# A decoder layer on one core: banded scores of two key parts in one matmul, gate loads issued a step earlier, and weight sums, a merge and the last feature's products put elsewhere

## The chip, the cores and the metric

The kernel runs on one core of a Trainium2 chip. A core has a matrix engine (TensorE, PE in the profile, with its weight loads as PEld), a vector engine (VectorE, DVE), a scalar engine (ScalarE, ACT), a general engine (GpSimd, POOL), a queue engine that issues most of the transfers (SyncE, SP), and sixteen DMA engines. Data lies in the on-chip memory SBUF, matmul results in PSUM, everything else in DRAM. The metric is the time of one execution on the device in microseconds (us); less is better.

## The reference

One layer of a decoder over 1024 tokens of width 1024, in float32, with 3 x 4 heads of dilated window attention beside 4 heads of differential attention, and a gated feed-forward part with a short causal convolution:

```python
h = rms_norm(x, pre_mix_g)
qa, ka, va, qb, kb, vb, gates = split(h @ w_in)          # 1024 x (512*3 + 1536*3 + 2048)
ya = (rms_norm(diff_attention(rope(qa), rope(ka), va, lam), diff_head_g) * (1 - lam_init)) @ w_a_out
for g, (window, dil) in enumerate(((128, 1), (512, 4), (2048, 16))):
    outs[g], lses[g] = dilated_group(rope(qb[g]), rope(kb[g]), vb[g], window, dil)
yb = sum_g(softmax_over_g(lses)[g] * outs[g]) @ w_b_out
g_a, g_b = split(sigmoid(gates))
x = x + rms_norm((g_a * ya + g_b * yb) @ w_mix_out, post_mix_g)
u = causal_depthwise_conv(rms_norm(x, pre_ffn_g) @ w_up, conv_w, conv_b)     # 2 x 2816 columns
x = x + rms_norm((gelu(gate(u)) * value(u)) @ w_down, post_ffn_g)
```

`dilated_group` lets a query see the keys at its distance 0, dil, 2 dil ... up to `window`. On each residue class this is a band in blocks of 128 keys: the query's own block and the one before it.

## The kernel before, in words

**Precision.** Every operand of a large matmul is kept as two tiles: a high part (a ScalarE copy that rounds, L149) and a low part (a VectorE subtraction of that from the source, L146). A product is three matmuls into one PSUM region (`mm3`, L155 to L157): high by high, low of the first by high, high of the first by low of the second. PE is so the engine that is always wanted, and ACT and DVE split, scale and drain for it.

**Order.** The work goes through the stages below, and inside them a planner (`interleave`, `later`, `due`) hands out pieces: attention of one step is interleaved with the projections of the next one; a piece put off with `later(n, ...)` is issued n matmul jobs later. Each engine then runs its own list in the order of issue and waits only where an operand or a buffer is not there.

1. Norms, tables, values, and attention A with its projections, up to about 500 us.
2. Attention B, about 505 to 855 us, in twelve steps of (pair, group g, head h), each over 4 pairs of query blocks (`attend_b`). Group 0 has keys of two blocks for nearly all query blocks, group 1 for every second one, group 2 (whose residue classes are folded in twos) always one block of 128. Scores of a pair stand in one PSUM bank `s`; DVE adds the mask and takes the largest (L992), ACT takes the exponential (L998), PE turns the result (L713), and ACT and DVE copy it into two parts; PE multiplies with the values (L725, L727) and ACT and DVE drain (`osb`, L1026 and L1027). Queries and keys of the next step come from `proj_b`: DVE turns them by the rotary tables, and ACT and DVE write the parts `qh`, `ql`, `kh`, `kl` (L894 and L895), one half of the sequence at a time. Where a step opens a new group, `between` splits that group's values into `vh` and `vl` between the query's and the key's projections. `put_stats` has PE turn a step's row sums for DRAM, with a copy `rows` on ACT (L1050).
3. Branch A output, about 855 to 925 us: `branch` loads weight units, loads two gate tiles ahead (`gl<-gt_d`, on POOL's queue), takes their sigmoid on ACT (L1188), and DVE multiplies each product by its gate (`ya`, L1210). Beside it run the pieces of the last heads' merge over groups (`merge`: loads of `mw` and `og`, one DVE product of 1536 columns, L1106, two sums L1107 and L1109), at the job numbers of the tuple (3, 5, 7, 11, 16).
4. Branch B output and the mix, then the up projection. Features 2 to 21 each take seven products of 12 matmuls (`seven`) in place of eight. Four of the seven weights are sums of weight quarters: `combined` starts a tile `s` and adds the others by DMAs on POOL's queue (L1408); `weights` then splits each into parts. The `s` tiles have four buffers, all four of one feature. Products p1, p2, p3 and p5 take the second operand straight out of the mix tiles `mh`, `ml`, products p6, p7 and p4 out of the separate tiles `t2`, `t3`, `t4`. Results go to `u` (L1446 first), through the convolution, and as `c` to DRAM (`c_d`).
5. The down projection, from about 1470 us, again by sevens: `load(n)` brings `ax` from `c_d` (L1570) and `by` from the weights (L1571) for the product "p1"; their places in SBUF are those of tiles that the up projection has used, `by`'s among them those of the mix tiles. Matmuls there are L1618 to L1620.

## Time and profile before

| what | us |
|---|---|
| three runs | 1689.71, 1692.87, 1689.78 |
| their median | 1689.78 |
| the profiled execution, its own time | 1693.0 |
| span of the profile (first to last instruction) | 1691.1 |
| PE busy / DVE busy / ACT busy / POOL busy | 1672.0 / 1318.6 / 923.9 / 161.9 |
| mean granted TensorE clock | 0.997 |

The profile is one execution. What a row of the timeline shows: start, duration, engine, line, operation, and output<-inputs by the program's names; in square brackets the time that the engine stood idle just before and what it waited for. Matmuls overlap, so what one costs is the distance from its start to the next one's start, not its duration. The 1.9 us between 1691.1 and 1693.0 lie around the span.

### The profile page before, as it was taken

Reading aid. Unit: us, or ns where it says so; the run is one execution under the profiler, and the core shown is the slowest. Engines: PE = TensorE matmul, PEld = TensorE weight load, DVE = VectorE, ACT = ScalarE, POOL = GpSimd, SP = SyncE. Lnnn points to the kernel's source line nnn. Section 1 sums busy time; section 2 is a strip of 40 time slices with the busy share of each in tenths; the row PEclk is TensorE's granted clock in tenths of the full one; section 3 lists DMA queues with packets and bytes.
Section 4 is the critical chain, followed back from the end, with each engine's and each line's share of the span. In section 5 each row is a group of like instructions: output and inputs, shape, how many; then the busy total and the mean of one; then the engine's idle time right before and its main releaser. Section 6 shows DMA issues by size and latency. Waiting matters only on the chain. (4 is left out here: it accounts for less than half of the span.)

```text
span 1691.1 us, 22909 instructions
## 1 busy us (share of the span) xinstructions
PE 1672.0 (99%) x7878; PEld 1395.7 (83%) x7878; DVE 1318.6 (78%) x2446; ACT 923.9 (55%) x1723; POOL 161.9 (10%) x251
## 2 busy tenths in 40 slices
PE   9999999999999999999999999999999999999997
PEld 7888888888888888888878888888888888878886
DVE  8794686877777777788866865988888778689978
ACT  7643575655554777667653533565555455255463
POOL 0031000000000000010123400022211121000000
PEclk9999999999999999999999999999999999999999
DMA  8777311214112122333676632267655655296524
GB/s 273 228 248 245 98 59 61 88 57 121 48 63 81 55 72 77 107 120 119 208 257 215 203 112 87 51 162 171 163 132 133 154 134 128 98 338 214 197 88 149
DMA packets 115973, 237.40 MB, mean 140 GB/s; under 512 B 14272, under 2 KB 23424, under 8 KB 115856
## 3 DMA queue, kind: packets, MB, share of 16 engines
q1 hardware_dynamic: 89296, 171.28, 30.4%
q0 software_dynamic: 21808, 56.26, 14.2%
q10 hardware_dynamic: 4752, 8.39, 1.3%
q8 instruction: 62, 1.02, 0.2%
q14 instruction: 55, 0.45, 0.1%
HBM read 177.54 MB, written 47.86 MB: 133 GB/s over the span
## 5 line engine op out<-in xcount | busy, mean ns | idle before, releaser
L157 PE MATMUL acc<-xl,whi 128*128 128x512 f32 x768 | 303.2, 395 | 0.0
L155 PE MATMUL acc<-xh,whi 128*128 128x512 f32 x768 | 302.1, 393 | 0.0
L156 PE MATMUL acc<-xh,wlo 128*128 128x512 f32 x768 | 301.9, 393 | 0.0
L149 ACT ACTIVATE whi<-raw 128x512 fp32r<-128x512 f32 (+1 forms) x249 | 153.9, 626 | 162.6 <-PE acc L157 94.2
L146 DVE TENSOR_TENSOR wlo<-raw,whi 128x512 fp32r<-128x512 f32 (+1 forms) x249 | 171.9, 698 | 27.8 <-ACT whi L149 23.5
L156 PEld LDWEIGHTS acc<-xh,wlo 128*128 128x128 f32 x768 | 144.6, 188 | 28.2
L157 PEld LDWEIGHTS acc<-xl,whi 128*128 128x128 f32 x768 | 144.6, 188 | 28.0
L155 PEld LDWEIGHTS acc<-xh,whi 128*128 128x128 f32 x768 | 144.7, 188 | 27.5
L155 PE MATMUL acc<-mh,whi 128*128 128x512 f32 x384 | 149.7, 390 | 1.4 <-ACT u L1446 1.1
L156 PE MATMUL acc<-mh,wlo 128*128 128x512 f32 x384 | 149.4, 389 | 0.0
L157 PE MATMUL acc<-ml,whi 128*128 128x512 f32 x384 | 149.1, 389 | 0.0
L700 ACT ACTIVATE t<-acc 64x512 f32<-64x512 f32 (+1 forms) x160 | 94.6, 591 | 60.1 <-PE acc L157 58.2
L149 ACT ACTIVATE whi<-s 128x512 fp32r<-128x512 f32 x80 | 49.8, 627 | 90.8 <-PE acc L157 68.7
L1442 DVE TENSOR_TENSOR u<-acc,u 128x512 f32<-128x512 f32 x100 | 68.4, 685 | 28.4 <-PE acc L157 28.2
L701 DVE TENSOR_TENSOR t<-acc,cos 128x512 f32<-128x512 f32 x64 | 44.2, 690 | 59.4 <-ACT t L700 58.9
L155 PEld LDWEIGHTS acc<-mh,whi 128*128 128x128 f32 x384 | 72.1, 188 | 17.4 <-ACT u L1446 2.0
L157 PEld LDWEIGHTS acc<-ml,whi 128*128 128x128 f32 x384 | 72.1, 188 | 15.0
L156 PEld LDWEIGHTS acc<-mh,wlo 128*128 128x128 f32 x384 | 72.1, 188 | 14.7
L1619 PE MATMUL acc<-whi,wlo 128*128 128x512 f32 x216 | 76.0, 390 | 0.0
L1618 PE MATMUL acc<-whi 128*128 128x512 f32 x216 | 74.9, 390 | 0.3 <-ACT whi L149 0.3
L1620 PE MATMUL acc<-wlo,whi 128*128 128x512 f32 x216 | 71.6, 390 | 0.0
L793 ACT ACTIVATE s<-s,mx 128x896 f32<-128x896 f32 (+7 forms) x64 | 49.3, 771 | 35.1 <-DVE mx L786 18.8
(403 smaller groups left out, 4033.9 us busy)
## 6 DMA issues: line engine op xcount, KB each, us to landing
raw<-in_w_in SPq DMA_DIRECT2D x96, 256.0 KB, 2.9
raw<-in_w_v SPq DMA_DIRECT2D x71, 256.0 KB, 5.0
raw<-in_w_up SPq DMA_DIRECT2D x68, 256.0 KB, 3.5
raw<-c_d SPq DMA_DIRECT2D x48, 256.0 KB, 3.7
c_d<-c SPq DMA_DIRECT2D x22, 512.0 KB, 3.9
s<-in_w_up POOLq DMA_DIRECT2D x40, 256.0 KB, 4.1
s<-s POOLq DMA_DIRECT2D x40, 256.0 KB, 3.9
raw<-in_w_down SPq DMA_DIRECT2D x37, 256.0 KB, 3.6
```

The costliest lines, as they stand in the source:

```text
L146: eng.tensor_tensor(lo, src, hi.bitcast(F32), op=ALU.subtract)
L149: copy = nc.scalar.activation(hi, src, AF.Copy)
L155: nc.tensor.matmul(o, sh, mh, start=first, stop=False, skip_group_check=on)
L156: nc.tensor.matmul(o, sl, mh, start=False, stop=False, skip_group_check=on)
L157: nc.tensor.matmul(o, sh, ml, start=False, stop=last, skip_group_check=on)
L700: nc.scalar.activation(t1[dst], ps[src], AF.Copy)
L701: nc.vector.tensor_tensor(t2, ps, cos[:, sl], op=ALU.mult)
L793: exp = nc.scalar.activation(sc[c][:, :w], sc[c][:, :w], AF.Exp, bias=mx[:, c, 0:1], scale=-1.0, accum_out=den[:, c : c + 1])
L1442: nc.vector.tensor_tensor(to, made(p), x, op=ALU.add)
L1618: nc.tensor.matmul(banks[m], gh[:, tk], wh, start=f == 0, stop=False)
L1619: nc.tensor.matmul(banks[m], gl[:, tk], wh, start=False, stop=False)
L1620: nc.tensor.matmul(banks[m], gh[:, tk], wl, start=False, stop=f == NH - 1)
```

## The change

It has six parts.

- **Scores.** For groups 1 and 2 the high and the low part of the keys lie in one tile `kp` of the shape (128, 2, 512), two such tiles for the two halves of the sequence. Where a query block has one key block, one matmul of the high query part over both (256 columns, L1009) and one of the low query part over the high keys (128 columns, L1010) take the place of the three of 128 columns. The columns of high by low then lie beside the others in PSUM; a new DVE addition (`low`, L1017) adds the mask to them, and the result stands in the place of the mask in the old reduction. Two-block scores and group 0 keep `mm3`. With two tiles, the key copies (L905 and L906) are issued for each half of a tile apart: four of 256 columns in place of two of 512, on ACT and on DVE.
- **Keys ahead.** The key copies are issued at a higher priority where the step has value splits. On ACT the order at the first such place stays: `vh_5509`, an `osb`, a `pt`, the `rows` copy, `vh_5513`, and then the key copies, four of them now and two before; DVE likewise has `vl` ahead of them.
- **Gates.** The first two gate tiles of branch A are loaded ahead of the last step of attention B and handed to `branch`. POOL's order of transfers around them is the one of before.
- **Merge.** The fourth number of the tuple goes from 11 to 12.
- **Weight sums.** Of odd features the four sums are made in one tile of the pool `early`, of even ones in the four `s` buffers. On POOL the sums of feature 4 now stand ahead of those of feature 3.
- **Last feature.** Its products go p1, p2, p3, p5, p6, p7, p4 (`LAST_UP` gives the weights in that order); before they went p1, p6, p2, p7, p5, p4, p3.

```diff
@@ -46,6 +46,7 @@
 NH = NF // 2
 AHEAD, T1_AT, LAST = 4, 5, 7
+LAST_UP = ("a11", "a12", "s4", "s1", "s2", "s3", "a22")
 MIX_UNITS = {3: (0,), 4: (1,), 5: (2, 4), 6: (5,), 7: (6, 3, 7)}
 START_GATES, A_FILLS, B_GATES = 1, ("gpgg", "gpvgg", "wgpgg", "xgPVgg"), 3
 SLOTS = 18
@@ -883,22 +884,38 @@
     def proj_b(g, h, res, between=None):
         dil = DIL[g]
-        qh, ql, kh, kl = (slot(n) for n in ("qh", "ql", "kh", "kl"))
-        res += [qh, ql, kh, kl]
+        qh, ql = (slot(n) for n in ("qh", "ql"))
+        if g == 0:
+            keys = [tuple(slot(n) for n in ("kh", "kl"))]
+        else:
+            keys = [slot("kp", (P, 2, 512)) for _ in range(2)]
+        res += [qh, ql, keys]
         n = 512 // dil
-        def put(hi, lo):
+        def pair_of(t):
+            return t if isinstance(t, tuple) else (t[:, 0], t[:, 1])
+
+        def put(*tiles):
             def evacuate(half, sl, ps):
                 t = rotated(ps, *tabs_b, sl, 64).rearrange("p (i r) -> p r i", r=dil)
-                o, l = (t_.rearrange("p (r i) -> p r i", r=dil)[:, :, half * n : (half + 1) * n] for t_ in (hi, lo))
-                nc.scalar.activation(o, t, AF.Copy)
-                nc.vector.tensor_tensor(l, t, o.bitcast(F32), op=ALU.subtract)
+                m = dil // len(tiles)
+                for x, pair in enumerate(tiles):
+                    o, l = (t_.rearrange("p (r i) -> p r i", r=m)[:, :, half * n : (half + 1) * n] for t_ in pair_of(pair))
+                    from_ = t[:, x * m : (x + 1) * m]
+                    nc.scalar.activation(o, from_, AF.Copy)
+                    nc.vector.tensor_tensor(l, from_, o.bitcast(F32), op=ALU.subtract)
             return evacuate
-        yield from proj_t(QB + g * 512 + h * P, put(qh, ql))
+        yield from proj_t(QB + g * 512 + h * P, put((qh, ql)))
         if between:
             between()
-        yield from proj_t(KB + g * 512 + h * P, put(kh, kl))
+        evacuate = put(*keys)
+
+        def first(*at):
+            with tc.high_priority(offset=80 if between else 0):
+                evacuate(*at)
+
+        yield from proj_t(KB + g * 512 + h * P, first)
     steps = [(pair, g, h) for pair in range(2) for g in range(BG) for h in (2 * pair, 2 * pair + 1)]
     ops_b = {s: [] for s in steps}
@@ -966,7 +983,7 @@
     def attend_b(g, h, jj, ops, vs, sbs):
-        qh, ql, kh, kl = ops
+        qh, ql, keys = ops
         scale = P ** -0.5
         if jj == 0:
             sbs.append(wk_b[0].tile([P, S], F32, tag="osb", name="osb", bufs=1))
@@ -980,17 +997,32 @@
             spans.append((j, kb, at))
             at += len(kb) * P
         ps = psum(F32, ps_s, "s")
-        for j, kb, a0 in spans:
-            w, k = slice(a0, a0 + len(kb) * P), slice(kb[0] * P, (j + 1) * P)
+        per = 8 // len(keys)
+        for n, (j, kb, _) in enumerate(spans):
+            kp = keys[j // per]
+            kh, kl = kp if g == 0 else (kp[:, 0], kp[:, 1])
+            k = slice(kb[0] % per * P, (j % per + 1) * P)
             qs = slice(j * P, (j + 1) * P)
-            mm3(ps[:, w], qh[:, qs], ql[:, qs], kh[:, k], kl[:, k], True, True)
+            w = ps[:, n * 2 * P : n * 2 * P + len(kb) * P]
+            if g and len(kb) == 1:
+                two = ps[:, n * 2 * P : (n + 1) * 2 * P].rearrange("p (t k) -> p t k", t=2)
+                nc.tensor.matmul(two, qh[:, qs], kp[:, :, k], start=True, stop=False)
+                nc.tensor.matmul(w, ql[:, qs], kh[:, k], start=False, stop=True)
+            else:
+                mm3(w, qh[:, qs], ql[:, qs], kh[:, k], kl[:, k], True, True)
+        masks = [mask_2 if g == 2 else mask_b[:, (2 - len(kb)) * P :] for _, kb, _ in spans]
+        n = sum(len(kb) == 1 for _, kb, _ in spans) if g else 0
+        if n:
+            low = wk_b[0].tile([P, 2, P], F32, tag="low", name="low", bufs=1)[:, :n]
+            nc.vector.tensor_tensor(low, ps.rearrange("p (n t k) -> p n t k", n=2, t=2)[:, :n, 1],
+                                    masks[0].unsqueeze(1).to_broadcast([P, n, P]), op=ALU.add)
+            masks[:n] = [low[:, x] for x in range(n)]
         s_sb = wk_b[0].tile([P, 512], F32, tag="bs", name="bs", bufs=2)
         at = [j % 2 * 4 + jj if g == 1 else j for j in (2 * jj, 2 * jj + 1)]
-        for j, kb, a0 in spans:
+        for n, (j, kb, a0) in enumerate(spans):
             w = slice(a0, a0 + len(kb) * P)
-            mask = mask_2 if g == 2 else mask_b[:, (2 - len(kb)) * P :]
-            most = nc.vector.tensor_tensor_reduce(out=s_sb[:, w], in0=ps[:, w], in1=mask, scale=-scale, scalar=3.0e38,
-                                                  op0=ALU.add, op1=ALU.min,
+            most = nc.vector.tensor_tensor_reduce(out=s_sb[:, w], in0=ps[:, n * 2 * P : n * 2 * P + len(kb) * P], in1=masks[n],
+                                                  scale=-scale, scalar=3.0e38, op0=ALU.add, op1=ALU.min,
                                                   accum_out=stat[:, 0, at[j % 2] : at[j % 2] + 1])
         marks["DVE"] = most.ins
         for j, kb, a0 in spans:
@@ -1152,6 +1184,9 @@
                 later(i, fn, 0)
+    gls = [tabs.tile([P, S], F32, tag=tag, name="gl") for tag in ("cos", "sin")]
+    for i, t in enumerate(gls):
+        side(t, gt_d[i])
     pair, g, h = steps[-1]
     oa = [[slot(n) for _ in range(AH)] for n in ("oah", "oal")]
     load_o(oa, None, 0, 1, ots[0])
@@ -1174,9 +1209,9 @@
     mid_b = open_pool(st_o, "mid_b")
     ob += [[mid_b.tile([P, S], F32R, tag=f"{n}{h}", name=n) for h in range(BH)] for n in ("obh", "obl")]
-    def branch(w_out, o, first, gate_tile, get_psum, scale=None):
-
-        gts = []
+    def branch(w_out, o, first, gate_tile, get_psum, scale=None, gts=()):
+
+        gts = list(gts)
         for d2 in range(KC // 2):
             wh, wl = load_unit(w_out[d2], scale=scale)
             for e in range(2):
@@ -1197,16 +1232,13 @@
     for h in range(2):
         load_o(ob, ob_d, h, 3 * h + 4)
-    for i, fn in zip((3, 5, 7, 11, 16), merge(BH - 1, ob)):
+    for i, fn in zip((3, 5, 7, 12, 16), merge(BH - 1, ob)):
         later(i, fn, 0)
-    first_gls = iter(("cos", "sin"))
-
     def gate_slot():
-        tag = next(first_gls, None)
-        return tabs.tile([P, S], F32, tag=tag, name="gl") if tag else slot("gl", dt=F32)
-
-    for d, half, sl, ps, gt in branch(a["w_a_out"], oa, 0, gate_slot, psum, ghead):
+        return slot("gl", dt=F32)
+
+    for d, half, sl, ps, gt in branch(a["w_a_out"], oa, 0, gate_slot, psum, ghead, gls):
         marks["DVE"] = nc.vector.tensor_tensor(ya[d][:, sl], ps, gt[:, sl], op=ALU.mult).ins
         clock[0] += 1
         while due and due[0][0] <= clock[0]:
@@ -1398,7 +1430,7 @@
         a11, a12, a22 = (load_raw(d, mid.tile([P, 512], F32, tag="r", name="raw", bufs=2) if f == FULL and d is not d22 else "raw") for d in (d11, d12, d22))
         def combined(name, first, *more):
-            t = mid.tile([P, 512], F32, tag="s", name=name, bufs=4)
+            t = other[:, "1324".index(name[1])] if f % 2 else mid.tile([P, 512], F32, tag="s", name=name, bufs=4)
             if first.space == DRAM:
                 dma(t, first)
             else:
@@ -1408,16 +1440,17 @@
                 nc.gpsimd.dma_start(t, x, accum_op=ALU.add)
             return t
+        other = early.tile([P, 4, 512], F32, tag="e", name="sums") if f % 2 else None
         s1 = combined("s1", d21, d22)
         minus_s3 = combined("s3", a11, d21)
         s2 = combined("s2", a11, s1)
         minus_s4 = combined("s4", a12, s2)
         return dict(a11=a11, a12=a12, s2=s2, s3=minus_s3, s1=s1, s4=minus_s4, a22=a22)
-    def weights(raws, *names):
+    def weights(raws, *names, order=()):
         ws = {}
-        for name in names or raws:
+        for name in names or order or raws:
             ws[name] = slot_w(wb if (name in ("s1", "s4", "a22") if names else len(ws) % 2) else None)
             split(*ws[name], raws[name])
         return ws
@@ -1530,8 +1563,8 @@
         if f + 1 == NF:
             for i in range(AHEAD):
                 put(i, load_raw(g_at(0, 0, i)), load_raw(w_at(0, 0, i)))
-        following = weights(fetch(f + 1)) if f + 1 < NF else None
-        gated(f, seven(f, ws, ("p1", "p2", "p7", "p6", "p3") if f == FULL else ()))
+        following = weights(fetch(f + 1), order=LAST_UP if f + 2 == NF else ()) if f + 1 < NF else None
+        gated(f, seven(f, ws, ("p1", "p2", "p7", "p6", "p3") if f == FULL else ("p1", "p2", "p3", "p5", "p6") if f + 1 == NF else ()))
         ws = following
     st_up.close()
     st_x.close()
```

On PE, scores of group 2 in one step: `s` is the PSUM bank, `acc` a projection's. Before:

```order
L156 MATMUL acc_6302<-xh_98,wlo_6233 128x512
L155 MATMUL s_6290<-kh_5941,qh_5939 128x128
L156 MATMUL s_6290<-kh_5941,ql_5940 128x128
L157 MATMUL s_6290<-kl_5942,qh_5939 128x128
L155 MATMUL s_6290<-kh_5941,qh_5939 128x128
L156 MATMUL s_6290<-kh_5941,ql_5940 128x128
L157 MATMUL s_6290<-kl_5942,qh_5939 128x128
```

The same bank with the change:

```order
L1009 MATMUL s_6310<-kp_5954,qh_5952 128x256
L1010 MATMUL s_6310<-kp_5954,ql_5953 128x128
L1009 MATMUL s_6310<-kp_5954,qh_5952 128x256
L1010 MATMUL s_6310<-kp_5954,ql_5953 128x128
L157 MATMUL acc_6401<-xh_98,wlo_6390 128x512
```

Six matmuls of 128 columns have become two of 256 and two of 128. There are 48 such query blocks, 16 in group 1 and 32 in group 2.

On DVE, the beginning of branch A: `ya` is a gated product of the branch, `mw` the 1536-column product of the merge. Before:

```order
L1210 TENSOR_TENSOR ya0_8633<-acc_8678,gl_8668 128x512
L141 SCALAR_TENSOR_TENSOR wlo_8868<-raw_8873,ghead_84,whi_8867 128x512
L1106 TENSOR_TENSOR mw_8492<-og_8496,mw_8492 128x1536
L1210 TENSOR_TENSOR ya1_8634<-acc_8714,gl_8670 128x512
L1027 TENSOR_TENSOR osb_8280<-osb_8280,o_8523 128x2x128
```

With the change:

```order
L1242 TENSOR_TENSOR ya0_8685<-acc_8726,gl_8320 128x512
L147 TENSOR_TENSOR pt_8604<-pt_8601,pt_8604 128x256
L1059 TENSOR_TENSOR osb_8332<-osb_8332,o_8497 128x2x128
L1242 TENSOR_TENSOR ya1_8686<-acc_8762,gl_8321 128x512
L1242 TENSOR_TENSOR ya0_8685<-acc_8776,gl_8320 128x512
L1138 TENSOR_TENSOR mw_8544<-og_8548,mw_8544 128x1536
```

The large product of the merge moved from behind the first `ya` to behind the third. A later one, that of the tuple's changed number, moves in the same way from behind the third of the four products of `ya4` and `ya5` to behind the last.

On SP, the entry of the down stage: `c_d<-c` is the store of the last feature, `ax` and `by` the operands of the down stage. Before:

```order
L1367 DMA c_d_94<-c_13670 128x1024
L1570 DMA ax_13884<-c_d_94 128x512
L1571 DMA by_13856<-in_w_down 128x512
L1570 DMA ax_13885<-c_d_94 128x512
L1571 DMA by_13857<-in_w_down 128x512
```

With the change:

```order
L1399 DMA c_d_94<-c_13688 128x1024
L1604 DMA by_13874<-in_w_down 128x512
L1604 DMA by_13875<-in_w_down 128x512
L1604 DMA by_13876<-in_w_down 128x512
L1604 DMA by_13877<-in_w_down 128x512
```

Eleven `by` loads now stand in a row, and the eleven `ax` loads follow them, where the two alternated.

## The prediction

> **What bounds the kernel now.** The page first:
>
> ```profile
> span 1691.1 us, 22909 instructions
> PE   1672.0 (99%) x7878; PEld 1395.7 (83%) x7878; DVE 1318.6 (78%) x2446; ACT 923.9 (55%) x1723; POOL 161.9 (10%) x251
> ```
>
> PE is busy for 99% of the span, so time can come from two places alone: the matmuls themselves, and the 19 us in which PE stands idle. The waits of PE say who ends those idle times; these are the rows that the edits can touch (in us: total, times, longest):
>
> ```profile
> PE pt L713 <- ACT rows L1050: 1.4, 1, 1.4
> PE o L725 <- DVE osb L1027: 1.2, 1, 1.2
> PE acc L155 <- ACT u L1446: 1.1, 2, 0.8
> PE pt L1618 <- ACT whi L149: 1.1, 1, 1.1
> PE acc L155 <- DVE ya L1210: 0.8, 1, 0.8
> PE s L157 <- DVE kl L895: 0.6, 1, 0.6
> ```
>
> They sum to 6.2 us: no removal of waits is worth more than this list, apart from short waits that it leaves out. One stretch stands out in the windows, by PEclk (the ninth number, the granted clock):
>
> ```profile
> 574.30:581.20 6.90, 6.33 (x26) 5.75 (x26) 6.90 (x15) 4.23 (x10) 0.00 (x0) 0.51 0.21 81
> ```
>
> At about half the clock, 6.9 us lose some 3.4 us. 1693.0 less 3.4 is 1689.6, which is what two of the three runs took (1689.71, 1689.78); the third, 1692.87, looks like the profiled execution. I read the median as a run without that stretch.
>
> **Scores merged.** Score matmuls of group 2, then of group 1, by their starts:
>
> ```profile
> 656.75 0.34 PE L725 MATMUL o<-pt,vh 128*128 128x256 f32 x1
> ...
> 656.99 0.33 PE L725 MATMUL o<-pt,vh 128*128 128x256 f32 x1
> ...
> 657.85 0.28 PE L155 MATMUL s<-kh,qh 128*128 128x128 f32 x1
> ...
> 658.08 0.28 PE L157 MATMUL s<-kl,qh 128*128 128x128 f32 x1
> 658.19 0.44 PE L157 MATMUL acc<-xl,whi 128*128 128x512 f32 x1
> ...
> 612.62 0.28 PE L156 MATMUL s<-kh,ql 128*128 128x256 f32 x1
> 612.74 0.28 PE L157 MATMUL s<-kl,qh 128*128 128x256 f32 x1
> ...
> 613.10 0.40 PE L156 MATMUL acc<-xh,wlo 128*128 128x512 f32 x1
> 613.33 0.39 PE L157 MATMUL acc<-xl,whi 128*128 128x512 f32 x1
> ```
>
> Three of 128 columns (the second left out) take 0.34, from 657.85 to 658.19, 0.113 each; one of 256 takes 0.12 (612.62 to 612.74), one of 512 takes 0.23 (613.10 to 613.33). So 128 columns cost nearly what 256 cost, and columns are not what they pay for. A pair of 256 and 128 columns with a weight load each, as the change makes it, stands in the rows of the value products: 0.24 from the start at 656.75, with its second matmul left out, to the next pair's at 656.99. The other way, 0.12 + 0.113 = 0.23. So each of the 48 merged blocks saves about 0.105 (between 0.34 - 0.24 and 0.34 - 0.23), together 48 x 0.105 = 5.0 us. The starts are rounded to 0.01, which leaves 4.5 to 5.5. I take -5.0.
>
> The Trainium skill, page "TensorE: Matmul & The Clock Gate", section "Back-to-back issue gap", gives for a matmul alone N/2.4 + 2.5 ns, by which 128 columns take 56 ns and the merge saves only one fixed part per block, an estimate of 0.1 us in all; its 81 ns for a stream of 128-column matmuls with weight loads would make the saving an estimate of 2.5 us. The 113 ns between the starts above disagree with both.
>
> What pays for it is DVE: 32 additions `low` and the key copies in halves. The reduction over the same PSUM sizes gives the price:
>
> ```profile
> L992 DVE CUSTOM_DVE_ANT_0 bs<-s,mask_b x50: 276/415/469, 573.8 to 794.2; 128x256 f32<-128x256 f32 x32, 128x128 f32<-128x128 f32 x18
> 570.00:850.00 280.00, 277.93 (x1477) 238.25 (x1476) 221.73 (x493) 195.52 (x421) 18.35 (x30) 0.99 0.35 116
> 770.00:790.00 20.00, 20.00 (x107) 16.99 (x106) 19.69 (x49) 15.25 (x32) 3.14 (x5) 1.00 0.32 101
> ```
>
> 16 additions of 128 columns at 0.28 and 16 of 256 at 0.42 are 11.2 us. With some 2 us for the copies' additional starts, an estimate, DVE goes from 221.7 to 235 of the 280 us between 570 and 850. It fits, and even in the fullest 20 us (19.69 busy) PE did not wait. I put this at 0, because PE always has a projection's matmuls between a score and its transpose; without that cover each addition would hold PE for its own length, and the upper end is the second rival. Below nothing it cannot go.
>
> **Keys.** At the entry of group 1 PE waits twice, 1.4 us for `rows` and 0.6 for `kl` in the list of waits:
>
> ```profile
> 570.74 1.04 ACT L149 ACTIVATE vh<-vperm 128x1024 fp32r<-128x1024 f32 x1
> ...
> 575.05 0.46 PE L155 MATMUL s<-kh,qh 128*128 128x128 f32 x1
> ...
> 575.58 2.08 DVE L895 TENSOR_TENSOR kl<-t,kh 128x512 fp32r<-128x512 f32 x2
> ...
> 576.73 0.47 PE L157 MATMUL s<-kl,qh 128*128 128x128 f32 x1 [0.57 <-DVE kl L895]
> ```
>
> The `rows` copy stood behind a value split (570.74, 1.04 us long). The edit means to put keys ahead of it, but in the order that split stays where it was, so this wait stays. At the second, four matmuls that need only `kh` ran from 575.05 on before PE stood. With the change the first score needs low keys too, so PE stands from 575.05 on, but only until the first half-copy is done, half of 2.08 / 2 after 575.58, at 576.1 instead of 576.7; the next block then needs the third of four half-copies, done at 577.1. I take 0, from -0.5 to +0.6, the present wait once less or once more.
>
> **Gates and merge.** The end of attention B and the first branch:
>
> ```profile
> 853.91 1.06 ACT L1188 ACTIVATE gl<-gl 128x1024 f32<-128x1024 f32 x1 [2.60 <-DMA gl<-gt_d]
> ...
> 868.47 1.76 DVE L1106 TENSOR_TENSOR mw<-og,mw 128x1536 f32<-128x1536 f32 x1 [2.66 <-DMA og<-og_d]
> ...
> 870.41 0.39 PE L157 MATMUL acc<-oal,whi 128*128 128x512 f32 x1
> 870.88 0.50 PE L155 MATMUL acc<-oah,whi 128*128 128x512 f32 x1
> ...
> 898.06 1.76 DVE L1106 TENSOR_TENSOR mw<-og,mw 128x1536 f32<-128x1536 f32 x1 [5.42 <-DMA mw<-e_d]
> ...
> 899.91 0.39 PE L155 MATMUL acc<-obh,whi 128*128 128x512 f32 x1
> ...
> 901.08 0.50 PE L155 MATMUL acc<-oah,whi 128*128 128x512 f32 x1 [0.78 <-DVE ya L1210]
> ```
>
> The sigmoid at 853.91 waited for its gate, with `osb` behind it on ACT, and `osb` is what PE waited for 1.2 us. POOL issues these loads in the same order as before, and the sigmoid stays ahead of `osb`: 0, at best -1.2. The two merge products kept DVE waiting for transfers (2.66 and 5.42) with a `ya` behind them, and PE lost 0.47 - 0.23 = 0.24 and 1.17 - 0.23 = 0.94, where 0.23 is the normal distance of two starts. Both products now stand behind a further `ya`, and by then their transfers, which do not move, have landed. What is late next is the `ya` after that, which has 2.7 us (12 matmuls) of PE behind it against 1.76 of DVE. I take -1.2, between -1.2 and 0.
>
> **Weight sums.** The wait for `u`, twice, 1.1 in all, has its cause on ACT:
>
> ```profile
> 1155.11 0.63 ACT L149 ACTIVATE whi<-s 128x512 fp32r<-128x512 f32 x1 [4.32 <-DMA s<-s]
> ...
> s<-s POOLq DMA_DIRECT2D x40, 256.0 KB, 3.9
> ```
>
> ACT holds the copy of p1 to `u` behind a split that waits for a sum. With eight buffers instead of four the sums of a feature can start a feature earlier, and both waits can go: -1.1. Against it: on POOL the sums of feature 4 overtake those of feature 3, whose tile `early` is free only after the split of `t1`. A chain of a weight's sums is two or three transfers of 3.9 us (last row, to landing) and has the length of a feature to land in, 7 x 12 x 0.23 = 19 us; where that is not enough, feature 3 waits as features 4 and 5 do now, 0.8 for the longest. I take -0.7, from -1.1 to +0.8.
>
> **Last feature.** The last products use `t2`, `t3`, `t4`, so the mix tiles are free after the fourth product instead of the seventh, three products of 12 x 0.23 = 8.3 us earlier, and SP can issue `by` that much sooner:
>
> ```profile
> 1470.24 0.33 SPq L1571 DMA_DIRECT2D by<-in_w_down  x1
> ...
> 1480.92 0.39 PE L1620 MATMUL acc<-wlo,whi 128*128 128x512 f32 x1
> ...
> 1481.05 0.63 ACT L149 ACTIVATE whi<-ax 128x512 fp32r<-128x512 f32 x1 [3.74 <-DMA ax<-c_d]
> ...
> 1482.41 0.50 PE L1618 MATMUL pt<-whi 128*128 128x512 f32 x1 [1.10 <-ACT whi L149]
> ...
> 1470.00:1515.00 45.00, 43.62 (x190) 35.06 (x189) 37.52 (x55) 22.34 (x36) 0.00 (x0) 1.00 0.89 318
> ```
>
> In this stretch the DMA engines are 0.89 busy at 318 GB/s. Eleven loads of 256 KB are 2.9 MB, 9 us at that rate, and they now run beside the last products. The fifth `ax`, for which the split of 1481.05 waited 3.74 us, then has no `by` ahead of it or beside it; it is due about 4 us sooner, an estimate (half of those 9 us). The wait of 1.49 - 0.23 = 1.26 goes, and what is late next is PE itself. I take -1.3, from -1.9 (short waits around 1512) to 0, if `ax` also has to wait for a buffer that the last product frees.
>
> **Sum.** -5.0 - 1.2 - 0.7 - 1.3 = -8.2. Against the profiled execution 1693.0 - 8.2 = 1684.8, with the stretch at half clock in it; without that, 1684.8 - 3.4 = 1681.4, and from the median 1689.78 - 8.2 = 1681.6. I take 1681.5.
>
> **Rivals.**
>
> *The half clock comes in the median run.* It came right after the waits at 572 and 576, of which the first stays and the second begins earlier. If two of three runs have it: 1681.5 + 3.4 = 1684.9. The Trainium skill, same page, section "Part 1: The HAM clock gate", says that an activity window of 3413 ns runs free of the kernel's start and halves the clock after an idle one; the stretch of 6.9 us agrees with two such windows. By this rule the kernel's phase against the window decides, so the same kernel can show both times, as the runs here do. Chance 0.3.
>
> *DVE takes PE's place in attention B* (the slower side). If the addition and the split copies push the masked scores past the transposes that PE has queued, PE waits in each group for what DVE was given: 11.2 + 2 = 13.2 us, and the time is 1689.8 - 8.2 + 13.2 = 1694.8. It decides from 8.2/32 = 0.26 us of wait per `low`. For it speaks 770 to 790 with DVE at 98%; against it that PE waited for no masked score in any of the steps there. Chance 0.06, and some 0.07 for half of it, 1688.1, the same within error.
>
> *Matmuls cost by their columns.* The merged block has the same 384 columns as before, so nothing is saved there and the remaining waits give 1689.8 - 3.2 = 1686.6. The starts 0.113 apart speak against it. It is what the Trainium skill, page "TensorE: Matmul & The Clock Gate", has for a matmul alone. Chance 0.05.
>
> *The change doesn't do what it says elsewhere*: sums, merge and last feature yield nothing, scores alone: 1689.8 - 5.0 = 1684.8. Chance 0.12.
>
> **How the numbers follow.** The forecast has 0.4. With the best ends of all terms (-5.5 - 0.5 - 1.2 - 1.2 - 1.1 - 1.9 = -11.4) one reaches 1689.8 - 11.4 = 1678.4, the low end; the high end at 1687.5 takes in the half clock, the scores alone, and the rival of columns, and leaves out the slower side. A measurement of this kernel can tell about 0.2%, 3.4 us, from no change: faster is below 1686.4, slower above 1693.2. Faster: 0.4 + 0.3 + 0.12 = 0.82; the same: 0.07 + 0.05 = 0.12; slower: 0.06.
>
> **What would show it.** PE's busy time in attention B falls by about 5 us with `s` matmuls of 256 columns 0.12 from the next start; the waits for `ya`, for `u` and for `whi` at the entry of the down stage are gone, those for `rows` and `osb` stay; `by` is issued near 1470.2 - 8.3 - 6.9 = 1455, before the last product ends. Wrong would be a 128-column matmul that still costs 0.11 behind a 256-column one that costs 0.2, a list of PE waits with `bs` or `low` in it, or a wait of feature 3 for its sums.

## The result, and where the time went

The changed kernel takes 1694.64 us (median of 10 runs, 1692.88 to 1700.66) against 1690.03 for the one before (10 runs): a ratio of 1.0028, with a 95% interval of 1.002 to 1.0037. It was forecast at 1681.5, so it came out 4.6 us slower where 8.2 us less were expected. The profiled executions took 1695.57 and 1693.0 us, only 2.6 us apart: that of the kernel before was slower than all ten of its timed runs. What follows compares these two. The page of the changed kernel, its first lines:

```profile
span 1693.8 us, 22894 instructions
...
PE 1670.6 (99%) x7830; PEld 1392.9 (82%) x7830; DVE 1325.9 (78%) x2494; ACT 924.6 (55%) x1739; POOL 163.1 (10%) x251
```

48 matmuls fewer, as the change says, 48 DVE instructions more, and PE busy nearly as long. The waits of PE, changed kernel:

```profile
PE acc L156 <- ACT whi L150: 4.0, 1, 4.0
PE o L726 <- DVE osb L1059: 2.2, 1, 2.2
PE pt L714 <- ACT rows L1082: 1.4, 1, 1.4
PE s L1009 <- DVE kp L906: 0.9, 1, 0.9
PE acc L156 <- ACT obh L150: 0.8, 1, 0.8
PE acc L156 <- DVE ya L1242: 0.5, 2, 0.3
```

The waits for `u` and for the split at the entry of the down stage are gone. Two others are new: 4.0 us for a split in the up projection, and 2.2 us for an `osb` in branch A where 1.2 stood. The windows give the granted clock (ninth number) in three stretches:

```profile
575.18:582.00 6.82, 5.97 (x23) 5.18 (x23) 6.82 (x14) 4.36 (x11) 0.00 (x0) 0.50 0.21 82
875.55:878.96 3.41, 3.41 (x10) 2.64 (x9) 3.41 (x7) 0.23 (x1) 0.00 (x0) 0.50 0.65 237
1117.90:1121.31 3.41, 3.41 (x9) 2.64 (x9) 3.41 (x7) 3.41 (x7) 0.00 (x0) 0.50 0.90 240
```

The first stood in the profile of before. The other two are new, and each begins right behind one of the two new waits. At half clock 3.41 us lose 1.7.

For an account I took every distance between two matmul starts and subtracted the cost by size (0.227 us for 512 columns, in proportion down to 0.111). What is over by more than 0.2 us is called a wait. Half the length of the half-clock stretches is lost to the clock. The rest is matmuls. Between the first and the last matmul, before and changed, in us:

| | before | changed | difference |
|---|---|---|---|
| matmuls | 1663.8 | 1658.2 | -5.6 |
| waits: start of the program | 4.9 | 6.1 | +1.2 |
| waits: keys, 571 to 578 | 2.6 | 2.9 | +0.3 |
| waits: end of attention B and branch A | 2.5 | 4.5 | +2.0 |
| waits: features 3 to 5 | 1.4 | 4.5 | +3.1 |
| waits: entry of the down stage | 1.7 | 0 | -1.7 |
| half clock | 3.4 | 6.8 | +3.4 |
| sum, with a wait of 0.5 at 1055 us in both | 1680.8 | 1683.5 | +2.7 |

So the matmuls gave what was forecast, and waits with the clock behind them took more than that. The waits at the start, which no part of the change touches, lie between 4.9 and 6.3 us in the profiles of this document, so the +1.2 is chance.

**The scores.** Two pairs of group 2 on PE in the changed kernel, by their starts:

```profile
657.55 0.28 PE L1009 MATMUL s<-kp,qh 128*128 128x256 f32 x1
657.66 0.22 PE L1010 MATMUL s<-kp,ql 128*128 128x128 f32 x1
657.72 0.34 PE L1009 MATMUL s<-kp,qh 128*128 128x256 f32 x1
657.89 0.22 PE L1010 MATMUL s<-kp,ql 128*128 128x128 f32 x1
657.96 0.45 PE L158 MATMUL acc<-xl,whi 128*128 128x512 f32 x1
```

The first pair takes 0.17 to the next start, the second 0.24: 0.41 for both, where each trio took 0.34. By the account above, the nine profiled kernels with merged scores have 1656.9 to 1660.1 us of matmuls and the five without 1662.4 to 1664.0; the means differ by 4.6 us.

**Feature 3.** SP, POOL, ACT and PE of the changed kernel around the 4.0 us:

```profile
1102.44 0.33 SPq L1435 DMA_DIRECT2D sums<-in_w_up  x1
1105.77 1.72 POOL L1440 DMA_DIRECT2D sums<-in_w_up  x2 [1.11 <-PE acc L158]
1109.87 0.87 POOL L1440 DMA_DIRECT2D s<-s  x1 [2.38 <-DMA s<-s]
1112.78 0.86 POOL L1440 DMA_DIRECT2D sums<-sums  x1 [2.04 <-DMA sums<-in_w_up]
1116.49 1.15 ACT L150 ACTIVATE whi<-sums 128x512 fp32r<-128x512 f32 x2 [0.45 <-DMA sums<-sums]
1117.18 0.50 PE L156 MATMUL acc<-t2h,whi 128*128 128x512 f32 x1 [4.04 <-ACT whi L150]
```

`sums` are feature 3's, `s` feature 4's. The second product of feature 3 needs a weight that is the sum of a sum: two transfers in a row. The first is issued at 1105.77 (it had waited for a buffer that PE held), an addition of feature 4 stands between (1109.87), the second is issued at 1112.78 and lands at about 1116.4. In the kernel before, the additions of feature 3 took the buffers that feature 4 now has, from 1089 us on:

```profile
1089.46 0.84 POOL L1408 DMA_DIRECT2D s<-in_w_up  x1 [4.35 <-ACT s L1406]
1091.39 0.86 POOL L1408 DMA_DIRECT2D s<-in_w_up  x1 [1.08 <-DMA s<-in_w_up]
```

**Branch A.** POOL, DVE and PE of the changed kernel:

```profile
865.83 0.76 POOL L1127 DMA_DIRECT2D og<-og_d  x1 [2.80 <-issue]
871.15 1.76 DVE L1138 TENSOR_TENSOR mw<-og,mw 128x1536 f32<-128x1536 f32 x1 [5.96 <-DMA og<-og_d]
...
873.49 0.61 DVE L1059 TENSOR_TENSOR osb<-osb,o 128x256 f32<-128x256 f32 x1
...
874.16 0.39 PE L726 MATMUL o<-pt,vh 128*128 128x256 f32 x1 [2.21 <-DVE osb L1059]
```

The merge's product waits 5.96 us for `og`, whose load POOL issued 2.4 us later than before:

```profile
863.41 0.76 POOL L1095 DMA_DIRECT2D og<-og_d  x1 [2.17 <-issue]
```

Behind the product on DVE, with one weight split between, now stands an output addition, where a gated product came first before. PE has one PSUM bank for these outputs: it waits until the addition is done, at 873.49 + 0.61.

### The profile page after: what moved, and what is told of

It reads as the page before. It is cut to its first block, busy times and chain, and to the rows that moved or that the text cites. A ratio compares the mean times of both kernels' runs of the same rounds, so it can differ in the third digit from the quotient of the medians.

```text
span 1693.8 us, 22894 instructions
## 1 busy us (share of the span) xinstructions
PE 1670.6 (99%) x7830; PEld 1392.9 (82%) x7830; DVE 1325.9 (78%) x2494; ACT 924.6 (55%) x1739; POOL 163.1 (10%) x251
## 5 line engine op out<-in xcount | busy, mean ns | idle before, releaser
L1651 PE MATMUL acc<-whi 128*128 128x512 f32 x216 | 82.9, 389 | 0.0
L1652 PE MATMUL acc<-whi,wlo 128*128 128x512 f32 x216 | 82.9, 389 | 0.0
L1653 PE MATMUL acc<-wlo,whi 128*128 128x512 f32 x216 | 79.2, 389 | 0.0
L787 DVE CUSTOM_DVE_ANT_0 s<-s,mask_a 128x512 f32<-128x512 f32 (+3 forms) x96 | 52.5, 554 | 18.0 <-PE s L785 14.5
```

The lines of the kernel that those rows point to most:

```text
L787: nc.vector.tensor_tensor_reduce(out=s_sb[:, c0:c1], in0=ps, in1=mask, scale=-scale, scalar=3.0e38, op0=ALU.add, op1=ALU.min, accum_out=mx ...
L1651: nc.tensor.matmul(banks[m], gh[:, tk], wh, start=f == 0, stop=False)
L1652: nc.tensor.matmul(banks[m], gl[:, tk], wh, start=False, stop=False)
L1653: nc.tensor.matmul(banks[m], gh[:, tk], wl, start=False, stop=f == NH - 1)
```

## The experiments

Theory 1: the merged scores save their 5 us of matmuls, and two new waits of PE eat them, each with the half clock behind it: the sums of feature 3, and the merge's products in branch A. Theory 2: the merged scores save nothing.

**scores_only**: before with the scores and key edits alone, here as a diff against the changed kernel; the last feature's order, too, is the one of before:

```diff
-        other = early.tile([P, 4, 512], F32, tag="e", name="sums") if f % 2 else None
...
-    gls = [tabs.tile([P, S], F32, tag=tag, name="gl") for tag in ("cos", "sin")]
-    for i, t in enumerate(gls):
-        side(t, gt_d[i])
...
-    for i, fn in zip((3, 5, 7, 12, 16), merge(BH - 1, ob)):
+    for i, fn in zip((3, 5, 7, 11, 16), merge(BH - 1, ob)):
```

> The kernel before with the scores edit and the key priority alone. Theory 1 (the merged scores save the 5 us of matmuls that were forecast, and the changed kernel loses them again to two new waits of PE, one for the weight sums of feature 3 and one at the entry of branch A): the matmul saving of 5 us is there, so is the branch A wait of about 2.4 us with its half clock if that wait comes from the scores edit, since the products of the merge stand ahead of an output addition here too; together 1688 to 1690 us, and no wait for the sums of feature 3. Theory 2 (merged scores save nothing, because matmuls cost by their columns or because VectorE's additions hold PE back): 1692 to 1695 us, with the pairs of 256 and 128 columns no closer than 0.33 us or with waits for low or bs in the list of PE.

Measured: 1690.29 us, ratio 1.0002 (0.9993 to 1.0011): neither gain nor loss. By the account the matmuls take 4.2 us less than before, and no wait of feature 3 is there. The new waits of PE stand in branch A:

```profile
PE acc L156 <- DVE ya L1242: 1.5, 2, 1.3
PE acc L156 <- DVE gl L1274: 1.4, 1, 1.4
PE acc L156 <- DVE osb L1059: 0.8, 1, 0.8
```

From 830 to 925 us it loses 5.1 us in waits, before 2.5. The order on DVE shows why: with this edit alone the merge's products stand as in the changed kernel, ahead of output additions. So the edit that saves the matmuls also moves the merge, 300 us later; how the planner comes to that is not shown. Theory 1 holds, except that several shorter waits stand in place of the one and no half clock lies behind them. One thing more: the order of the last feature is the old one here, and yet PE does not wait at the entry of the down stage. In the stretch where before had 43.62 us of PE in 45, it is busy throughout:

```profile
1470.00:1515.00 45.00, 44.98 (x197) 36.56 (x196) 40.12 (x60) 24.19 (x40) 0.00 (x0) 1.00 0.94 341
```

**rest_only**: the complement, the changed kernel with `proj_b` and `attend_b` of before.

> The changed kernel without the scores and the key copies (those as before), all else changed. Theory 1: the 5 us that the merged scores save are missing, the wait at feature 3 is there, the wait for an output addition at the entry of branch A is not (on VectorE the merge's product stands behind a gated product again): about 1690.0 + 6.1 - 1.4 - 1.7 = 1693 us, no more than 2 us less than the changed kernel. Theory 2 (the merged scores lose time): below 1690 us.

Measured: 1694.71 us, ratio 1.0031 (1.0019 to 1.0042), as slow as the whole change. The losing half of the change needs no scores:

```profile
PE acc L156 <- ACT whi L150: 4.2, 1, 4.2
...
PE o L726 <- DVE osb L1028: 2.0, 1, 2.0
```

The `osb` wait stands at 856 to 858 us, where 1.2 us stood before, and for the same cause: `osb` is queued on ACT behind the sigmoid of the third gate, which waits for its transfer:

```profile
855.81 1.06 ACT L1192 ACTIVATE gl<-gl 128x1024 f32<-128x1024 f32 x1 [2.94 <-DMA gl<-gt_d]
856.78 0.61 ACT L1027 ACTIVATE osb<-o 128x256 f32<-128x256 f32 x1
```

Loading the first two gates a step earlier does nothing for the third. Both waits have a half-clock stretch of 3.41 us behind them. The wait for `osb` was not expected here; with it the time is 1.7 us above the forecast of 1693.

**no_sums**: the changed kernel with all sums in the four `s` buffers.

```diff
-            t = other[:, "1324".index(name[1])] if f % 2 else mid.tile([P, 512], F32, tag="s", name=name, bufs=4)
+            t = mid.tile([P, 512], F32, tag="s", name=name, bufs=4)
...
-        other = early.tile([P, 4, 512], F32, tag="e", name="sums") if f % 2 else None
```

> The changed kernel with all weight sums in the four s buffers again. Theory 1: the wait of 4.0 us before the second product of feature 3 goes, with the half clock behind it (1.7 us); the two waits of the kernel before at features 4 and 5 (1.4 us together) come back: 1694.6 - 6.1 + 1.4, about 1690 us. Theory 2 (the sums are not the loss, the wait would fall elsewhere in the up projection): 1693 to 1695 us.

Measured: 1689.52 us, ratio 0.9997 (0.9988 to 1.0006), 5.1 us less than the changed kernel. The wait is gone and the forecast of 1690 met. The waits at features 4 and 5 that were to come back are not in the profile, whose execution took 1685.86 us and has no half clock; branch A has 4.4 us of waits there. Without the early tile the rest of the change measures as no change.

**flip**: the early tile for the even features from 4 on instead.

```diff
-            t = other[:, "1324".index(name[1])] if f % 2 else mid.tile([P, 512], F32, tag="s", name=name, bufs=4)
+            t = other[:, "1324".index(name[1])] if f % 2 == 0 and f > FULL else mid.tile([P, 512], F32, tag="s", name=name, bufs=4)
...
-        other = early.tile([P, 4, 512], F32, tag="e", name="sums") if f % 2 else None
+        other = early.tile([P, 4, 512], F32, tag="e", name="sums") if f % 2 == 0 and f > FULL else None
```

> The changed kernel with the early tile for the sums of the even features from 4 on, the s buffers for the others, so that feature 3 starts its sums where the kernel before starts them. Theory 1 (feature 3 waits because its tile comes free late and because the additions of feature 4 stand ahead of its own): neither the wait at feature 3 nor those at features 4 and 5 is there, 1694.6 - 6.1, about 1688.5 us. A rival (any sum in the early tile comes too late there): a wait of 2 to 4 us moves to feature 4, 1692 to 1695 us.

Measured: 1689.53 us, ratio 1.0 (0.9991 to 1.0008). The wait of 4 us is gone, but two shorter ones, in feature 4, stand at 1129 and 1135:

```profile
PE acc L156 <- ACT whi L150: 0.7, 1, 0.7
PE acc L156 <- DVE u L1475: 0.5, 1, 0.5
```

So the second set of buffers costs nothing here, and gains nothing against one set.

**in_order**: the changed kernel with POOL's additions of feature 4 behind those of feature 3.

```diff
+                with tc.issue_after(third[-1]) if f == FULL + 2 else nullcontext():
-                nc.gpsimd.dma_start(t, x, accum_op=ALU.add)
+                    done = nc.gpsimd.dma_start(t, x, accum_op=ALU.add)
+                if f == FULL + 1:
+                    third.append(done.ins)
```

> The changed kernel with one thing added: POOL issues the additions of feature 4 behind those of feature 3. Theory 1a (the wait at feature 3 is mostly the queue: the second sum of feature 3 was ready to be added at about 1110 us and was issued at 1112.8, behind an addition of feature 4 that waited for its own transfer): the wait of 4.0 us shrinks to 1 to 1.5 us and the half clock behind it goes, 1694.6 - 4.5, about 1690 us. Theory 1b (it is mostly the tile, which comes free at about 1105 us only): the wait stays at 3 us or more, 1693 to 1694.5 us.

Measured: 1700.9 us, ratio 1.0065 (1.0051 to 1.0078), against both. The profiled execution took 1697.61 us, so its rows do not account for the whole of it. POOL and PE there:

```profile
1102.83 1.73 POOL L1443 DMA_DIRECT2D sums<-in_w_up  x2 [19.74 <-PE acc L158]
1108.89 0.84 POOL L1443 DMA_DIRECT2D sums<-sums  x1 [4.33 <-DMA sums<-in_w_up]
1112.84 0.85 POOL L1443 DMA_DIRECT2D sums<-sums  x1 [2.99 <-ACT whi L150]
1113.46 2.02 POOL L1443 DMA_DIRECT2D s<-in_w_up  x2
...
1112.89 0.50 PE L156 MATMUL acc<-t2h,whi 128*128 128x512 f32 x1 [2.58 <-ACT whi L150]
```

The second sum is issued 3.9 us earlier (1108.89), but PE still waits 2.6 us: the queue is a part of the 4.0, the tile, free at 1102.8 in this run, the larger. And the additions of feature 4, which now stand in the queue from 1083 us behind a tile that isn't free, start 23 us later (1113.46; 1090.22 in the changed kernel). In feature 4 PE then waits 2.5 us, at 1134, and 1.9 us, at 1143. A split of the 4.0 between queue and tile beyond this is not shown.

**merge_out**: the changed kernel without the merge's product and sums for heads 2 and 3; their output is a constant.

```diff
-            nc.vector.tensor_tensor(wt, og, wt, op=ALU.mult)
...
+            if to is None:
+                nc.vector.tensor_tensor(wt, og, wt, op=ALU.mult)
...
+            else:
+                nc.vector.memset(o, 0.5)
```

> The changed kernel without the merge's product and sums for heads 2 and 3 (their output is a constant), so that nothing on VectorE in branch A waits for the transfers of og and mw. Theory 1 (the waits at 872, 875, 903 and 916 us come from these products standing ahead of output additions and gated products while their transfers are on the way): those four waits, 4.1 us in the profile, and the half clock behind the first (1.7 us) go, 1694.6 - 5.8, about 1689 us. Theory 2 (PE waits there for ScalarE's sigmoid or for the weights): 1693 to 1695 us.

Measured: 1688.74 us, ratio 0.9989 (0.9981 to 0.9998). 5.9 us less than the changed kernel, and between 830 and 925 us no wait of PE is over 0.2 us. It shows that the waits hang on these products. It takes out their work on DVE together with their waits for transfers, so it does not tell the two apart; s3, next, keeps both.

**s3**: before with scores, keys and the last feature's order, and three pieces of the merge one to three jobs later.

```diff
-    for i, fn in zip((1, 2, 3, 5, 9), merge(2, ob)):
+    for i, fn in zip((1, 2, 3, 8, 11), merge(2, ob)):
...
-    for i, fn in zip((3, 5, 7, 11, 16), merge(BH - 1, ob)):
+    for i, fn in zip((3, 5, 7, 12, 16), merge(BH - 1, ob)):
```

> The kernel before with the scores, the key priority, the last feature's order, and the merge's pieces two to three jobs later (1, 2, 3, 8, 11 and 3, 5, 7, 12, 16), so that the products of the merge stand behind gated products with another gated product next, not an output addition. Theory 1: the scores' 4.5 us and the last feature's 1 us are kept and branch A loses no more than before (2.5 us): 1689.9 - 5, about 1685 us. Theory 2 (branch A loses time wherever those products stand, because their transfers land late): 1688 to 1690 us.

Measured: 1684.67 us, ratio 0.9964 (0.9952 to 0.9976): faster than both kernels. The window of the branch (its length and PE's busy time first), and then the waits of PE that are left in the middle of the program:

```profile
850.00:925.00 75.00, 75.00 (x339) 61.99 (x338) 51.86 (x82) 36.81 (x53) 21.56 (x30) 1.00 0.73 249
```

```profile
PE pt L714 <- ACT rows L1082: 1.4, 1, 1.4
PE s L1009 <- DVE kp L906: 1.3, 1, 1.3
PE acc L156 <- ACT u L1478: 1.2, 1, 1.2
```

PE is busy in all of branch A, though the merge's products and transfers are all there. So it is their place that decides, not that they are done. The changed kernel less what no_sums and merge_out took off (5.1 and 5.9) would be 1683.6, an estimate; s3, which has neither loss, comes within 1.1 us of it.

**io_s3**: in_order with the merge's pieces at 8 and 11.

> The run in_order with the merge's first pieces at 8 and 11 in place of 5 and 9. Theory 1: 3 to 4 us less than in_order, since the waits of branch A at 872 to 916 us (4.1 us) fall to those of the kernel before: about 1686 us if in_order gives 1690. Theory 2 (late transfers, wherever the products stand): the same as in_order within 1 us.

Measured: 1695.99 us, ratio 1.0032 (1.002 to 1.0044), 4.9 less than in_order, where 3 to 4 were forecast; the waits of branch A sum to 1.0 instead of 3.7. So the gain came, but not the time: 1686 was forecast, with in_order at 1690.

**last_only**: before with the last feature's order alone.

```diff
-        following = weights(fetch(f + 1)) if f + 1 < NF else None
+        following = weights(fetch(f + 1), order=LAST_UP if f + 2 == NF else ()) if f + 1 < NF else None
...
-        gated(f, seven(f, ws, ("p1", "p2", "p7", "p6", "p3") if f == FULL else ()))
+        gated(f, seven(f, ws, ("p1", "p2", "p7", "p6", "p3") if f == FULL else ("p1", "p2", "p3", "p5", "p6") if f + 1 == NF else ()))
```

> The kernel before with the last feature's order alone. Theory 1 (this edit is worth the wait for ax at the entry of the down stage and the short one behind it, 1.26 + 0.42 us): 1688.1 us against 1689.8, no wait of PE for a split at the entry of the down stage. Theory 2 (the eleven loads of by put ahead delay ax as much as they are issued sooner): the wait for ax stays, 1689.8 us.

Measured: 1689.53 us, ratio 0.9995 (0.9986 to 1.0004). The profile has no wait at the entry of the down stage, where that of before had 1.7 us. But neither have scores_only and late_b, which keep the old order, so the wait of before did not come in every execution. The timing can tell the edit neither from 1.7 us nor from nothing: what it is worth is not shown.

**late_b** and **late**: the value splits called after the key projection, in the kernel before (shown) and in flip.

```diff
-        if between:
-            between()
         yield from proj_t(KB + g * 512 + h * P, put(kh, kl))
+        if between:
+            between()
```

> The kernel before with only that: value splits called after the key projection. Theory 1: the waits at 571 and 576 us, 2.6 us together, go and the half clock behind them (3.4 us in the profile of before) with them: 1689.8 - 2.6 - 2 to 3.4, 1684 to 1685 us. Theory 2 (the half clock comes for another reason): 1687 us, with a stretch at half clock near 575 us all the same.

> The kernel of the run flip, with the value splits called after the key projection, so that in the order of ScalarE and VectorE the key copies really stand ahead of them. Theory 1 (the waits at 572 and 576 us come from the value splits, and the half clock behind them is theirs): 1.5 + 0.3 + 1.4 us of waits and 1.7 to 3.4 us of half clock go, 1689.5 - 5, about 1684.5 us. Theory 2 (the splits are only late elsewhere: the first value product of the next group waits for them instead): 1688 to 1690 us with a wait of PE for vh or vl.

late_b: 1688.03 us, ratio 0.9985 (0.9976 to 0.9994). Waits and half clock at 571 to 581 are gone:

```profile
570.00:580.00 10.00, 10.00 (x64) 8.94 (x63) 4.00 (x11) 5.30 (x15) 0.00 (x0) 1.00 0.10 30
```

It gains 2.6 us on the median of before that was measured beside it (1690.59), of the 5 us expected. By the account, waits of 0.9 us at 587 and of 1.7 us together at 912 and 918 come in part of their place. late: 1693.08 us, ratio 1.0014 (1.0005 to 1.0023), 3.6 more than flip, of which 0.8 lies between the medians of before that were measured beside the two. With the merged scores' additions the same edit loses; two rows of PE in late, and two of its waits:

```profile
588.03 0.36 PE L1009 MATMUL s<-kp,qh 128*128 128x256 f32 x1 [0.83 <-DVE stat L1024]
...
589.88 0.55 PE L714 MATMUL pt<-ident,bs 128*128 128x128 f32 x3 [1.02 <-DVE pt L147]
```

```profile
PE acc L156 <- DVE t L702: 2.0, 1, 2.0
PE acc L156 <- ACT obh L150: 3.9, 2, 2.7
```

Between 587 and 593 PE waits three times for DVE, 4.4 us, with `vl`, `low` and the reductions queued there; in branch A PE waits 5.7 us in three waits, and the half clock behind one wait in each place takes 5.1 us. It was expected to be 1684.5; neither theory had DVE as the place.

**lateb_last**: late_b with the last feature's order.

> The kernel before with the value splits behind the key projection and the last feature's order, without merged scores. Theory 1 (the two gains add: 2.5 us as measured for the splits, 1.1 us for the last feature): 1690.0 - 3.6, about 1686.5 us. A rival (the gains are the same half clock counted twice): 1688 us, as with the splits alone.

Measured: 1686.95 us, ratio 0.9979 (0.997 to 0.9988). That is 1.1 us below late_b, as forecast if the gains add, but the two intervals overlap and late_b's profile has no wait at the entry of the down stage that the order could remove. So that the gains add is not shown.

## Why the prediction was wrong

Three steps of the sum failed: the term for the weight sums, the term for gates and merge, and the half clock, which had no term for new waits. Together they were forecast at -1.9 us and came to +8.5 in the profiles.

The steps that rest on rows of the operation itself came out. **Scores**: -5.0 forecast, -5.6 in the profile and -4.2 in scores_only. The rival that matmuls cost by their columns falls. The Trainium skill's N/2.4 + 2.5 ns (page "TensorE: Matmul & The Clock Gate", section "Back-to-back issue gap"), which the page gives for a single matmul by itself, is no price for these, each of which loads weights. **Keys**: 0 forecast, +0.3; the wait for `rows` stayed, as the order said. What DVE was given in attention B is 11.0 us (232.7 against 221.7 of 280), of 13 forecast, and all of it but a wait of 0.2 us at 831 was hidden.

**Last feature**: -1.3 forecast, and the profiles differ by -1.7. `by` was issued when the fourth product ended, as the prediction said (1467.30, later than 1455, since the stages ahead had lost time instead of gaining it). But the wait is also absent in two kernels without the edit, so that the number came out may be luck.

Wrong was, first, the step on **weight sums**: "feature 3 waits as features 4 and 5 do now, 0.8 for the longest". -0.7 forecast, +3.1 measured. I took an upper end from another feature's wait, instead of following the chain at the place. There the tile is free at about 1105, then come two additions in a row of about 4 us each and a split, and PE is at the second product by 1112.98 (the start at 1112.75 plus 0.23). That would have given 1105 + 8 + 0.6, at least 0.6 us of wait, and with one addition of feature 4 between, some 4. I even named the overtaking and the tile, and a wait of feature 3 among the signs of being wrong, and priced neither.

Second, **gates and merge**: "by then their transfers, which do not move, have landed". -1.2 forecast, +2.0 measured. The transfers did move, 2.4 us later at POOL, and the product came to stand ahead of an output addition, with a single bank to cover it, where I had looked at the gated product behind it alone. I had also put the move of the later products down to the tuple's number; with 11 left there, all four stand on DVE where the change has them. It is the scores edit that moves them (scores_only).

Third, the **half clock** was a rival for the old stretch alone. A term of the sum was missing: each wait that is long enough brings 1.7 us more. Two new waits made it 3.4 us. The rule that I quoted from the Trainium skill (page "TensorE: Matmul & The Clock Gate", section "Part 1: The HAM clock gate") fits the rows: stretches of 3.41 us, and 300.37 and 242.35 us between their starts, 88.0 and 71.0 windows of 3.413 us. I used it to split the odds of one stretch and did not ask it of the waits that my own bounds allowed. Nor could the median of before be read as a run without a stretch. The three profiles without one show a mean granted clock of 0.999, that of before 0.997. Of the 77 timed runs of before beside the experiments, 11 show 0.999 and 38 show 0.997 or less.

The rival on the slower side, DVE in place of PE in attention B, was not what happened in the change. It happens in late, where the waits at 571 to 578 are gone.

## What to carry to other kernels

A second set of buffers helps only if it is free earlier than the first set is; give the tile that comes free late to the work that is due late, and look which queue the overtaking work shares. Where a wait is possible, follow its chain at that place to a time, and add half of the clock's window for each wait that is as long as those that brought a slow stretch. An edit under a planner is priced on the order that is built, for stages far behind it too: the saving of 5 us was lost 300 us later (scores_only), and with three other job numbers and the last feature's order the time fell by 5.6 us (s3). A wait that one profile shows need not be there in the next execution: look for it in the profiles of other kernels that leave its place alone.

## What the runs showed of the clock

Over the profiles of the thirteen kernels other than the one before, between 100 and 1600 us, 11 single waits of PE of 2.2 us or more stood, and each of the 11 had a half-clock stretch behind it, of 3.41 or 6.83 us. No shorter single wait had one (the longest is 2.03 us, in no_sums, at 897). The three waits of 571 to 577, about 3 us in 5 us of time, had one in before, changed, scores_only, rest_only, flip, merge_out, last_only and s3, and none in no_sums, in_order and io_s3, where they are as long.

What decides, as far as these traces show, is how the waits fall on a grid of 3.413 us. Within a profile all half-clock stretches, the one at the end of the program among them, start whole multiples of it apart (574.34 and 1687.09 us in before are 326.0 apart), and the grid lies elsewhere in each profile. Laid on the grid of their profile, the waits fill 1.8 us or more of 16 windows that are not at half clock already, and behind each of the 16 the clock was halved. Between 1.5 and 1.8 us it was so for 3 of 14, below that for none. The free-running window of the Trainium skill (page "TensorE: Matmul & The Clock Gate", section "Part 1: The HAM clock gate") agrees with this, with one thing to add from these runs: PE need not stand for the whole window, 1.8 of 3.4 us were enough. No run here sets the phase of the grid.
